# Seven-product blocks that add up in shared PSUM banks, in both column halves of three chunks out of eight

## The chip, the core and the metric

The kernel runs on one core of a Trainium2 chip, in one launch. The metric is device time in microseconds (us). Before the change three runs gave 2297.48, 2298.36 and 2298.86 us; the median is 2298.36 us.

Engine names are those of the profile: PE is TensorE (matrix products into PSUM), PEld its weight loads, DVE is VectorE, ACT is ScalarE, POOL is GpSimd, SP is the queue that starts the transfers from HBM. Nearly every instruction is recorded under one helper's line, L71, so the text goes by tile names.

## The reference, cut to what matters

A trunk of two layers on 256 tokens of width 2048: a mixer and a feed-forward block each, with residual sums. The change touches the two feed-forward blocks alone:

```
def squared_relu_mlp(h, w_up, w_down):
    u = jnp.einsum('bsd,df->bsf', h, w_up)
    return jnp.einsum('bsf,fd->bsd', jnp.square(jax.nn.relu(u)), w_down)
...
h = rms_norm(x, norm_ffn[layer])
x = x + squared_relu_mlp(h, w_up[layer], w_down[layer])
```

`w_up` is 2048 x 8192, `w_down` 8192 x 2048, all in float32.

## The kernel before

**Pieces.** All weights stream through the core once. The host-side list `plan` holds pieces of two row tiles (2 x 128 rows) by 512 columns, 512 KB each. SP loads a piece (`wraw`, four buffers, or `sraw`, from the shared pool of 29 slots). Float32 precision is made from three reduced products: ACT writes a rounded copy `whi` (`high`), DVE writes the rest `wlo` = raw - `whi` (`low`), and the PE adds up x_hi·w_hi, x_hi·w_lo and x_lo·w_hi. A plain piece is 12 matmuls of 512 columns (2 row tiles x 2 token halves x 3) into a pair of PSUM banks called `acc`.

**Order around a piece.** In step i of the loop in `run`, the queues get `low(i+2)` on DVE, the load of piece i+6 on SP, `high(i+3)` on ACT, `add(i+4)` on DVE (below), then what the piece before left behind (`pending`: an eviction), then side tasks that `tick` lets in, then the PE's piece i. There are four `wlo` buffers, so `low(j)` can't start until the PE is through with piece j-4: DVE is never more than some three pieces ahead. Engines take their queues in order.

**Feed-forward.** `up(i)` makes block i of 512 hidden columns (8 pieces; 16 blocks). `squared(i)` applies relu on ACT, turns the block with 8 PE transposes (`uT`) and squares it into `uf`. `operands(c)` splits blocks 2c and 2c+1 into `uh`/`ul` and makes two combinations of them, `s1` and `s2`, split into `sh`/`sl`. Chunk c (c = 0..7) multiplies the two blocks by 1024 rows of `w_down`. Column tiles 2 and 3 are plain: `down(c, 2)`, `down(c, 3)`, four pieces each, evicted by `add_stripe` into `res`.

**Seven products.** Column tiles 0 and 1 of chunks 0 to 6 go by a seven-product scheme (Winograd's form of Strassen's): the 2 x 2 blocks of token halves, hidden blocks and column tiles need seven products in place of eight. `Seven` gives 14 pieces, P1, P2, Q3, Q5, Q7, Q6, Q4 in two halves each, of 6 matmuls a piece into one bank, `sp`. Four of the seven weights are sums of raw blocks, made in place on DVE (`sraw<-sraw`, `add`). Each product is taken out of PSUM by one DVE addition (or, in chunk 0, an ACT copy), partly into the keeps `pq` and `q6`; after chunk 6 `together` combines these into `res` on DVE, and the first two column tiles of chunk 7 wait for that (`pre`). Chunk 7 is plain in all four column tiles.

**Plan.** Chunk c's stretch mixes its 14 seven-pieces into `up(2c+2)`, `down(c,2)`, `down(c,3)`, `up(2c+3)`, from the fifth of these pieces on. `operands(c)` waits for chunk c-1 to be through (`("seven", ...)`, `("rest", ...)`). So blocks 14 and 15 get their `uh`/`ul` only after the last piece of chunk 6, and `down(7, 0)` follows directly.

Of the kernel before, what the change touches and what calls it, by code (L numbers as in the profile page):

```python
# [7 lines left out]
F32 = mybir.dt.float32  # L8
# [3 lines left out]
OP = mybir.AluOpType  # L12
# [8 lines left out]
W = 512  # L21
# [19 lines left out]
def trunk(ctx: ExitStack, tc: tile.TileContext, x, norm_mix, norm_ffn, w_up, w_down, ab_w_in, ab_q_norm,  # L41
# [41 lines left out]
    def aux(name):  # L83
        return auxs.tile([128, W], F32, name=name, tag="aux")
# [150 lines left out]
    def unit(*a, **k):  # L235
# [1 line left out]

    SEVEN = (("P1", "11", None), ("P2", "21", None), ("Q3", "22", None), ("Q5", "11", "12"), ("Q7", "12", "22"),  # L240
             ("Q6", "11", "22"), ("Q4", "11", "21"))

    class Seven:


        def __init__(self, w, rows, c0, kts, operands, evict, needs, mark):
            self.w, self.rows, self.c0, self.operands, self.evict, self.needs, self.mark = \
                w, rows, c0, operands, evict, needs, mark
            self.halves = kts // KC
            self.raw = {}  # L250
            self.pieces = [(self, (p, h)) for p in range(7) for h in range(self.halves)]

        def fetch(self, p, h):
            _, block, other = SEVEN[p]
            b = block if other is None else "12" if p == 3 else None
            if b is not None:
                r, c = self.rows[int(b[0]) - 1] + h * KC, self.c0 + (int(b[1]) - 1) * W
                self.raw[b, h] = t = work.tile([128, KC, W], F32, name="sraw", tag="w4")
                nc.sync.dma_start(t, self.w[r * 128:(r + KC) * 128, c:c + W].rearrange("(k p) c -> p k c", p=128))

        def add(self, p, h):
            _, block, other = SEVEN[p]
            if other is not None:
                t = self.raw[block, h]
                V.tensor_tensor(t, t, self.raw[other, h], op=OP.add)

        def source(self, p, h):
            return self.raw[SEVEN[p][1], h]

    def run():  # L270
        todo = plan
# [50 lines left out]
        high(AHEAD)  # L322
        nc.sync.dma_start(cst[:, C_TRI:], shapes[:, C_TRI:])
        pending = []
        before = ps = sp = None
        kept, held = [], []
        for i, (u, c) in enumerate(todo):
            if i:
# [7 lines left out]
            hi, lo = parts.pop(i)  # L336
            if isinstance(u, Seven):
                p, h = c
                name = SEVEN[p][0]
                if p in u.needs and h == 0:  # L340
                    need(u.needs[p])
                if h == 0:
                    sp = aux("sp")
                xh, xl, t0 = u.operands(name)
                tick(True)
                for k in range(KC):
                    q = h * KC + k
                    wh, wl = xh[:, q, t0:t0 + 128], xl[:, q, t0:t0 + 128]
                    PE.matmul(sp, wh, hi[:, k], start=q == 0, stop=False)
                    PE.matmul(sp, wh, lo[:, k], start=False, stop=False)  # L350
                    PE.matmul(sp, wl, hi[:, k], start=False, stop=q == u.halves * KC - 1)
                if h == u.halves - 1:
                    pending.append(lambda u=u, name=name, sp=sp: u.evict(name, sp))
                    if p == 6:
                        done.add(u.mark)
                continue
# [238 lines left out]
                last(t, j)  # L595
        free(ps)

    def residual_unit(w, ktiles, j, needs={}, nm=None, last=None, pre=None, mark=None):
        def after(ps):
            if pre is not None:  # L600
                need(pre)
# [323 lines left out]
    def mlp(layer, nm, nxt, last=None):  # L925
# [21 lines left out]

        def operands(c):

            if c:  # L950
                yield from until(("seven", layer, c - 1))
                yield from until(("rest", layer, c - 1))
            for i in (2 * c, 2 * c + 1):
                yield from until(("uf", layer, i))
                u[i] = slot("uh"), slot("ul")
                split(u[i][0], u[i][1], uf[i])
                done.add(("u", layer, i))
                yield 2
# [20 lines left out]
        def up(i):  # L979
            return Unit([(wu, i * W, W)], nm.ktiles(), lambda ps: after_up(i, ps),  # L980
                        needs=nm.needs() if i == 0 else {}).pieces

        def down(c, j):
            kts = [(4 * (2 * c + b) + k, (lambda b=b, k=k: u[2 * c + b] + (k,))) for b in range(2) for k in range(4)]
            end = c == NC - 1
            return residual_unit(wd, kts, j, {4 * b: ("u", layer, 2 * c + b) for b in range(2)},
                                 nxt if end else None, last if end else None,
                                 ("seven's sums", layer) if end and j < 2 else None,
                                 ("rest", layer, c) if j == NS - 1 else None).pieces


        keep = {}
        R = [[res[:, t, j * W:(j + 1) * W] for j in range(2)] for t in range(2)]

        def evict(c, name, ps):
            if c == 0 and name == "P1":
                keep["pq"], keep["q6"] = w4([128, 2, W], "pq"), w4([128, W], "q6")
                keep["P1"], keep["Q5"], keep["Q6"] = keep["pq"][:, 0], keep["pq"][:, 1], keep["q6"]
                V.tensor_tensor(R[1][0], R[1][0], R[1][1], op=OP.add)
            if name in keep and c == 0:  # L1000
                S.activation(keep[name], ps, AF.Copy)
            else:
                r = {"P2": R[0][0], "Q3": R[0][1], "Q4": R[1][0], "Q7": R[1][1]}.get(name)
                r = keep[name] if r is None else r
                V.tensor_tensor(r, ps, r, op=OP.add)
            if c == NC - 2 and name == "Q4":
                side(together(), ("seven's sums", layer))

        def together():
            P1, Q5, Q6 = keep["P1"], keep["Q5"], keep["Q6"]  # L1010
            V.tensor_tensor(R[0][0], P1, R[0][0], op=OP.add)
            V.tensor_tensor(P1, Q6, P1, op=OP.subtract)
            V.tensor_tensor(R[1][1], P1, R[1][1], op=OP.add)
            V.tensor_tensor(R[1][0], R[1][0], R[1][1], op=OP.subtract)
            yield 2
            V.tensor_tensor(P1, P1, Q5, op=OP.add)
            V.tensor_tensor(R[0][1], P1, R[0][1], op=OP.add)
            V.tensor_tensor(R[1][1], Q5, R[1][1], op=OP.add)
            yield 1

        def seven(c):
# [20 lines left out]

# [113 lines left out]
```

## Time and profile before

| what | us |
|---|---|
| median of three runs | 2298.36 |
| the profiled execution's own time | 2297.73 |
| its span, first to last instruction | 2295.9 |
| PE busy | 2277.0 |
| DVE busy | 1692.5 |
| ACT busy | 1239.9 |

The page gives busy times and shares; the granted PE clock was 0.998 of full speed on average. The feed-forward blocks begin at 510.54 us and 1615.88 us (the first matmul of `up(0)`); the first one's last piece begins at 1186.68 us. A chunk takes 86.2 us. In the timelines a row's first number is a start, the second a length; rows of PE overlap (a matmul lasts 0.39 us, the next starts 0.23 us after it), so for PE the differences of starts count, and for DVE too, where an instruction of 1.22 us is followed 1.14 us after its start.

### The profile page before, as it was taken

The numbers are of one execution on the slowest core, as the hardware profiler recorded it, in microseconds if no ns is written. First come the engines' busy times: TensorE is split into PE (matmuls) and PEld (weight loads), VectorE is DVE, ScalarE is ACT, GpSimd is POOL, SyncE is SP. The second block draws the span as 40 slices with busy tenths as digits, with TensorE's granted clock in tenths as the row PEclk, the third lists the DMA queues.
The fourth block names the chain that finished last, engine by engine and source line by source line (L and its number), as shares of the span: only waits on it lengthen the run. The fifth ranks groups of instructions, "written<-read, shape, count | busy, mean of one in ns | idle before, by whom it ended". The sixth has DMA issues, their size and how long they took to land.

```text
span 2295.9 us, 29951 instructions
## 1 busy us (share of the span) xinstructions
PE 2277.0 (99%) x11149; PEld 1898.3 (83%) x11149; DVE 1692.5 (74%) x2418; ACT 1239.9 (54%) x1561; POOL 8.4 (0%) x20
## 2 busy tenths in 40 slices
PE   8999999999999999999999999999999999999998
PEld 7998988888888888888788778778888888888887
DVE  6779976556787787787866766665577787787785
ACT  5565554445556556556454555555555555555553
POOL 1000000000000000000000000000000000000000
PEclk9999999999999999999999999999999999999999
DMA  7546565566556656656456455545756656656654
GB/s 232 166 139 193 174 186 173 191 186 222 187 176 223 187 177 222 188 177 222 145 177 190 148 162 160 173 156 178 221 163 217 206 164 217 205 164 218 204 165 145
DMA packets 229202, 424.73 MB, mean 185 GB/s; under 512 B 15620, under 2 KB 26160, under 8 KB 229056
## 3 DMA queue, kind: packets, MB, share of 16 engines
q1 hardware_dynamic: 218976, 416.34, 58.1%
q10 hardware_dynamic: 9568, 6.34, 0.9%
q8 instruction: 87, 1.43, 0.2%
q14 instruction: 59, 0.48, 0.1%
q0 software_dynamic: 512, 0.15, 0.0%
HBM read 420.64 MB, written 2.13 MB: 184 GB/s over the span
## 4 chain that ended last, share of the span: by engine, by line
PE 98%; DVE 1%; DMA 0%; ACT 0%; issue 0%; SPq 0%; ACTq 0%
PE acc L71 81%; PE sp L71 12%; PE uT L71 1%; PE sc L71 1%; PE o L71 1%; PE pT L71 1%; PE yp L71 1%; PE xT L71 1%; DMA wraw<-in_ab_w_in_dram 0%; DVE res L71 0%; PE qp L71 0%; DVE wlo L71 0%; PE yo L71 0%; PE kp L71 0%; PE yT L71 0%; PE xtok L71 0%
## 5 line engine op out<-in xcount | busy, mean ns | idle before, releaser
L71 ACT ACTIVATE whi<-wraw 128x1024 fp32r<-128x1024 f32 (+1 forms) x680 | 717.4, 1056 | 641.4 <-PE acc L71 518.1
L71 DVE TENSOR_TENSOR wlo<-wraw,whi 128x1024 fp32r<-128x1024 f32 (+1 forms) x680 | 823.4, 1216 | 314.7 <-PE acc L71 227.5
L71 PE MATMUL acc<-whi,hThi 128*128 128x512 f32 (+1 forms) x1632 | 645.5, 396 | 2.6 <-ACT hThi L71 2.6
L71 PE MATMUL acc<-whi,hTlo 128*128 128x512 f32 (+1 forms) x1632 | 634.7, 389 | 0.3 <-DVE hTlo L71 0.3
L71 PE MATMUL acc<-wlo,hThi 128*128 128x512 f32 (+1 forms) x1632 | 633.9, 388 | 0.0
L71 PEld LDWEIGHTS acc<-whi,hThi 128*128 128x128 f32 x1632 | 307.6, 189 | 68.1 <-issue 5.9
L71 PEld LDWEIGHTS acc<-whi,hTlo 128*128 128x128 f32 x1632 | 307.3, 188 | 64.7 <-DVE hTlo L71 0.9
L71 PEld LDWEIGHTS acc<-wlo,hThi 128*128 128x128 f32 x1632 | 307.8, 189 | 60.4 <-issue 1.0
L71 ACT ACTIVATE whi<-sraw 128x1024 fp32r<-128x1024 f32 x196 | 207.7, 1060 | 178.4 <-DVE sraw L71 151.1
L71 DVE TENSOR_TENSOR wlo<-sraw,whi 128x1024 fp32r<-128x1024 f32 x196 | 239.7, 1223 | 59.4 <-PE acc L71 30.4
L71 PE MATMUL acc<-whi,uh 128*128 128x512 f32 x576 | 228.7, 397 | 3.4 <-ACT uh L71 3.4
L71 PE MATMUL acc<-whi,ul 128*128 128x512 f32 x576 | 226.0, 392 | 1.7 <-DVE ul L71 1.7
L71 PE MATMUL acc<-wlo,uh 128*128 128x512 f32 x576 | 225.5, 391 | 0.0
L71 DVE TENSOR_TENSOR sraw<-sraw 128x1024 f32<-128x1024 f32 x112 | 136.6, 1220 | 0.0
L71 PEld LDWEIGHTS acc<-whi,ul 128*128 128x128 f32 x576 | 108.9, 189 | 25.7 <-DVE ul L71 2.6
L71 PEld LDWEIGHTS acc<-whi,uh 128*128 128x128 f32 x576 | 108.9, 189 | 25.4 <-ACT uh L71 3.8
L71 PEld LDWEIGHTS acc<-wlo,uh 128*128 128x128 f32 x576 | 109.0, 189 | 21.7
L71 PE MATMUL acc<-hThi,whi 128*128 128x256 f32 x384 | 112.3, 293 | 0.0
L71 PE MATMUL acc<-hThi,wlo 128*128 128x256 f32 x384 | 108.5, 283 | 0.0
L71 PE MATMUL acc<-hTlo,whi 128*128 128x256 f32 x384 | 108.5, 283 | 0.0
L71 PE MATMUL sp<-whi,sh 128*128 128x512 f32 x224 | 87.1, 389 | 0.0
L71 PE MATMUL sp<-wlo,sh 128*128 128x512 f32 x224 | 87.1, 389 | 0.0
(228 smaller groups left out, 2535.9 us busy)
## 6 DMA issues: line engine op xcount, KB each, us to landing
wraw<-in_w_up_dram SPq DMA_DIRECT2D x256, 512.0 KB, 3.7
wraw<-in_w_down_dram SPq DMA_DIRECT2D x144, 512.0 KB, 4.3
sraw<-in_w_down_dram SPq DMA_DIRECT2D x112, 512.0 KB, 5.9
wraw<-in_ab_w_in_dram SPq DMA_DIRECT2D x96, 512.0 KB, 3.7
wraw<-in_c_w_qkv_dram SPq DMA_DIRECT2D x96, 512.0 KB, 4.0
wraw<-in_ab_w_out_dram SPq DMA_DIRECT2D x48, 512.0 KB, 3.7
wraw<-in_c_w_o_dram SPq DMA_DIRECT2D x32, 512.0 KB, 3.7
wt<-cumd ACTq DMA_DIRECT2D x8, 512.0 KB, 6.5
```

The costliest lines, as they stand in the source:

```text
L71: return f(out, *a, **k)
```

## The change

**Signs and banks.** `s1` and `s2` are made with their signs turned, and the order of the products is P1, P2, Q6, Q7, Q5, Q4, Q3. P1, Q6, Q5 and Q3 add up in one PSUM bank ("a"), Q7 and Q4 in another ("c"); P2 has one of its own. After each product DVE adds the bank as it stands to a block of `res`, or subtracts it. The keeps, `together` and the wait `pre` are gone, and so are ACT's copies in chunk 0.

**Weight sums.** P2 brings three raw blocks in one go (SP), and its own step makes the sum 11+12; Q6 needs 11+12+22 in a new tile `t2`, Q7 12+22, Q4 21-sum. As before, a seven has eight sums (four, in two halves each); P1, Q5 and Q3 have none.

**Both halves.** In chunks 0, 2 and 4 a second seven takes column tiles 2 and 3, so these chunks have no plain `down`. To have enough other pieces, they get three `up` blocks, and chunks 1, 3 and 5 get one.

**Order.** In chunk 6's stretch both `up` blocks come ahead of the plain `down` pieces, and `operands(7)` waits only for its own last block. The new `mixed` spreads the seven-pieces evenly.

```diff
-    SEVEN = (("P1", "11", None), ("P2", "21", None), ("Q3", "22", None), ("Q5", "11", "12"), ("Q7", "12", "22"),
-             ("Q6", "11", "22"), ("Q4", "11", "21"))
+    SEVEN = (("P1", "a", "11"), ("P2", "b", "21"), ("Q6", "a", "t2"), ("Q7", "c", "12"), ("Q5", "a", "11"),
+             ("Q4", "c", "21"), ("Q3", "a", "22"))
+    LOADS = {"P1": ("11",), "P2": ("21", "12", "22")}
+    SUMS = {"P2": ("11", "11", "12"), "Q6": ("t2", "11", "22"), "Q7": ("12", "12", "22"), "Q4": ("21", "21", "t2")}
...
+        def fetch(self, p, h):
...
+            for b in LOADS.get(SEVEN[p][0], ()):
...
+        def add(self, p, h):
...
+            if SEVEN[p][0] in SUMS:
+                o, x, y = SUMS[SEVEN[p][0]]
+                x, y = self.raw[x, h], self.raw[y, h]
+                V.tensor_tensor(self.raw[o, h] if o != "t2" else self.tile(o, h), x, y, op=OP.add)
...
+        def evict(self, p):
+
+            name, b, _ = SEVEN[p]
+            t, j, op = {"P1": (0, 0, OP.add), "P2": (0, 0, OP.add), "Q6": (1, 0, OP.add), "Q7": (1, 1, OP.subtract),
+                        "Q5": (1, 1, OP.subtract), "Q4": (1, 0, OP.add), "Q3": (0, 1, OP.subtract)}[name]
+            r = self.to[t][j]
+            V.tensor_tensor(r, r, self.bank[b], op=op)
...
-                if h == 0:
-                    sp = aux("sp")
+                new = b not in u.bank
+                if new:
+                    u.bank[b] = aux("sp")
+                sp = u.bank[b]
...
-                    PE.matmul(sp, wh, hi[:, k], start=q == 0, stop=False)
+                    PE.matmul(sp, wh, hi[:, k], start=new and k == 0, stop=False, skip_group_check=True)
...
-            if c:
-                yield from until(("seven", layer, c - 1))
-                yield from until(("rest", layer, c - 1))
+            if 0 < c < NC - 1:
+                for k in marks[c - 1]:
+                    yield from until(k)
+            if c == NC - 1:
+                yield from until(("uf", layer, 2 * c + 1))
...
-            V.tensor_tensor(s1[:, :, n], a1[:, :, o], s1[:, :, o], op=OP.subtract)
+            V.scalar_tensor_tensor(s1[:, :, n], a1[:, :, o], -1.0, s1[:, :, o], op0=OP.mult, op1=OP.subtract)
...
+        def mixed(rest, s, start):
+
+            n, k = len(s), 0
+            for i, x in enumerate(rest):
+                while k < n and i >= start + (len(rest) - start) / n * k:
+                    plan.append(s[k])
+                    k += 1
+                plan.append(x)
+            plan.extend(s[k:])
...
         plan.extend(up(0) + up(1))
-        for c in range(NC - 1):
-            rest = up(2 * c + 2) + down(c, 2) + down(c, 3) + up(2 * c + 3)
-            s = seven(c)
-            for k, x in enumerate(rest):
-                while s and k >= 4.5 + (len(rest) - 4.5) / 14 * (14 - len(s)):
-                    plan.append(s.pop(0))
-                plan.append(x)
-            plan.extend(s)
+        for c, (ups, both) in enumerate((((2, 3, 4), 1), ((5,), 0), ((6, 7, 8), 1), ((9,), 0), ((10, 11, 12), 1),
+                                         ((13,), 0), ((14, 15), 0))):
+            p = [up(i) for i in ups]
+            d = [] if both else [down(c, 2), down(c, 3)]
+            order = p[:1] + d + p[1:] if c < NC - 2 else p + d
+            mixed(sum(order, []), seven(c, 0) + (seven(c, 2) if both else []), 4.5)
```

How the instructions of the built programs stand, at two places.

DVE in chunk 0 of layer 0, from the splits of the two combinations on. Before, 12 rows from there:

```order
L71 TENSOR_TENSOR sl<-s_5336,sh 128x1024
L71 TENSOR_TENSOR sl<-s_5337,sh 128x1024
L71 TENSOR_TENSOR wlo<-wraw,whi 128x1024
L71 TENSOR_TENSOR wlo<-sraw,whi 128x1024
L71 TENSOR_TENSOR res<-res 128x512
L71 TENSOR_TENSOR wlo<-wraw,whi 128x1024
L71 TENSOR_TENSOR wlo<-sraw,whi 128x1024
L71 TENSOR_TENSOR wlo<-wraw,whi 128x1024 x2
L71 TENSOR_TENSOR wlo<-sraw,whi 128x1024
L71 TENSOR_TENSOR res<-sp,res 128x512
L71 TENSOR_TENSOR wlo<-wraw,whi 128x1024
L71 TENSOR_TENSOR wlo<-sraw,whi 128x1024
```

and in the changed kernel, from the row that stands just ahead of the same splits:

```order
L71 TENSOR_TENSOR sraw<-sraw 128x1024
L71 TENSOR_TENSOR sl<-s_5345,sh 128x1024
L71 TENSOR_TENSOR sl<-s_5346,sh 128x1024
L71 TENSOR_TENSOR wlo<-wraw,whi 128x1024
L71 TENSOR_TENSOR wlo<-sraw,whi 128x1024
L71 TENSOR_TENSOR sraw<-sraw 128x1024
L71 TENSOR_TENSOR res<-res,sp 128x512
L71 TENSOR_TENSOR wlo<-wraw,whi 128x1024
L71 TENSOR_TENSOR sraw<-sraw 128x1024
L71 TENSOR_TENSOR wlo<-sraw,whi 128x1024 x2
L71 TENSOR_TENSOR sraw<-sraw 128x1024
L71 TENSOR_TENSOR res<-res,sp 128x512
```

Four sums `sraw<-sraw` now stand around the splits and the first evictions of the seven, where the kernel before has none in its twelve rows.

DVE at the end of chunk 6 of layer 0. Before, from the last seven-product on:

```order
L71 TENSOR_TENSOR res<-sp,res 128x512
L71 TENSOR_TENSOR res<-pq,res 128x512
L71 TENSOR_TENSOR pq<-q_5412,pq 128x512
L71 TENSOR_TENSOR res<-pq,res 128x512
L71 TENSOR_TENSOR res<-res 128x512
L71 TENSOR_TENSOR wlo<-wraw,whi 128x1024
L71 TENSOR_TENSOR pq<-pq 128x512
L71 TENSOR_TENSOR res<-pq,res 128x512 x2
L71 TENSOR_TENSOR ul<-uf,uh 128x1024 x2
L71 TENSOR_TENSOR wlo<-wraw,whi 128x1024 x4
```

and in the changed kernel, from the eviction ahead of the first `ul` of block 14 on:

```order
L71 TENSOR_TENSOR res<-res,sp 128x512
L71 TENSOR_TENSOR wlo<-sraw,whi 128x1024
L71 TENSOR_TENSOR wlo<-wraw,whi 128x1024
L71 TENSOR_TENSOR ul<-uf,uh 128x1024
L71 TENSOR_TENSOR wlo<-wraw,whi 128x1024
L71 TENSOR_TENSOR res<-acc,res 128x512 x2
L71 TENSOR_TENSOR wlo<-sraw,whi 128x1024
L71 TENSOR_TENSOR res<-res,sp 128x512
L71 TENSOR_TENSOR ul<-uf,uh 128x1024
L71 TENSOR_TENSOR wlo<-wraw,whi 128x1024
L71 TENSOR_TENSOR wlo<-sraw,whi 128x1024
L71 TENSOR_TENSOR wlo<-wraw,whi 128x1024 x3
```

The two `ul`, which stood last, behind all of `together`, now stand between pieces of chunk 6, and the seven instructions of `together` are gone.

PE at the same place, before:

```order
L71 MATMUL acc<-wlo,hThi 128x512
L71 MATMUL acc<-whi,hTlo 128x512
L71 MATMUL uT<-cst,relu 128x128 x8
L71 MATMUL acc<-whi,uh 128x512
L71 MATMUL acc<-wlo,uh 128x512
```

and in the changed kernel, around the second set of block 15's transposes:

```order
L71 MATMUL sp<-wlo,sh 128x512
L71 MATMUL sp<-whi,sl 128x512
L71 MATMUL uT<-cst,relu 128x128 x4
L71 MATMUL acc<-whi,uh 128x512
L71 MATMUL acc<-wlo,uh 128x512
```

The transposes of the last block stood right ahead of the first product that needs them; now they stand between pieces of chunk 6, whose plain products use blocks 12 and 13.

## Rows read from the trace of the kernel before

**Rows 1.** The profile page: its first line, and the line of part 1 with busy time, share of the span and instructions of each engine.

```profile
span 2295.9 us, 29951 instructions
...
PE 2277.0 (99%) x11149; PEld 1898.3 (83%) x11149; DVE 1692.5 (74%) x2418; ACT 1239.9 (54%) x1561; POOL 8.4 (0%) x20
```

**Rows 2.** The waits of PE over the whole span, longest in total first: us in total, times, longest.

```profile
PE acc L71 <- ACT uh L71: 3.4, 2, 1.7
...
PE acc L71 <- ACT hThi L71: 2.6, 2, 2.3
PE acc L71 <- DVE ul L71: 1.7, 2, 0.9
```

**Rows 3.** Timeline of PE in chunk 6 of layer 0: the first matmul of a plain piece, of the seven-piece two plain pieces later, and of the next plain piece.

```profile
1108.19 0.39 PE L71 MATMUL acc<-whi,hThi 128*128 128x512 f32 x1
...
1113.63 0.39 PE L71 MATMUL sp<-whi,sh 128*128 128x512 f32 x1
...
1114.99 0.39 PE L71 MATMUL acc<-whi,hThi 128*128 128x512 f32 x1
```

**Rows 4.** Timeline of PE at the end of chunk 6, layer 0 (the last matmul of the last `up` piece, the transposes, the first products of chunk 7) and, after the dots, of layer 1 (the last matmul of the last `up` piece and, later, the twelfth product of chunk 7).

```profile
1136.52 0.39 PE L71 MATMUL acc<-whi,hTlo 128*128 128x512 f32 x1
...
1137.69 0.98 PE L71 MATMUL uT<-cst,relu 128*128 128x128 f32 x7 [0.35 <-ACT relu L71]
1140.36 0.50 PE L71 MATMUL acc<-whi,uh 128*128 128x512 f32 x1 [1.68 <-ACT uh L71]
...
1141.95 0.80 PE L71 MATMUL acc<-whi,ul 128*128 128x512 f32 x1 [0.86 <-DVE ul L71]
...
1145.09 0.39 PE L71 MATMUL acc<-whi,uh 128*128 128x512 f32 x1
...
2241.86 0.39 PE L71 MATMUL acc<-whi,hTlo 128*128 128x512 f32 x1
...
2251.04 0.39 PE L71 MATMUL acc<-whi,ul 128*128 128x512 f32 x1
```

**Rows 5.** Windows at the end of chunk 6, layer 0: length, busy us (and count) of PE, PEld, DVE, ACT, POOL, granted PE clock, DMA share, GB/s.

```profile
1136.70:1141.70 5.00, 2.25 (x11) 1.18 (x10) 4.93 (x7) 4.36 (x7) 0.00 (x0) 0.99 0.38 129
1141.70:1145.10 3.40, 3.15 (x8) 2.49 (x9) 2.47 (x3) 0.49 (x1) 0.00 (x0) 0.51 0.08 27
```

**Rows 6.** The same columns for chunks 1 and 2 of layer 0 together.

```profile
623.00:795.70 172.70, 172.70 (x779) 143.04 (x778) 136.27 (x131) 96.63 (x101) 0.00 (x0) 1.00 0.62 196
```

**Rows 7.** Timeline of DVE in the sums' stretch of chunk 1, layer 0.

```profile
663.88 0.68 DVE L71 TENSOR_TENSOR res<-sp,res 128x512 f32<-128x512 f32 x1
664.48 1.22 DVE L71 TENSOR_TENSOR wlo<-wraw,whi 128x1024 fp32r<-128x1024 f32 x1
665.61 1.22 DVE L71 TENSOR_TENSOR wlo<-sraw,whi 128x1024 fp32r<-128x1024 f32 x1
666.75 1.22 DVE L71 TENSOR_TENSOR sraw<-sraw 128x1024 f32<-128x1024 f32 x1
667.88 1.22 DVE L71 TENSOR_TENSOR wlo<-wraw,whi 128x1024 fp32r<-128x1024 f32 x1
669.17 1.22 DVE L71 TENSOR_TENSOR wlo<-sraw,whi 128x1024 fp32r<-128x1024 f32 x1
```

**Rows 8.** Timeline of DVE at the start of chunk 0, layer 0 (543 to 565 us).

```profile
543.47 1.22 DVE L71 TENSOR_TENSOR wlo<-wraw,whi 128x1024 fp32r<-128x1024 f32 x1
544.61 0.69 DVE L71 TENSOR_TENSOR s<-uf 128x512 f32<-128x512 f32 x1
...
547.14 1.22 DVE L71 TENSOR_TENSOR wlo<-sraw,whi 128x1024 fp32r<-128x1024 f32 x1
548.28 1.22 DVE L71 TENSOR_TENSOR wlo<-wraw,whi 128x1024 fp32r<-128x1024 f32 x1
550.04 2.36 DVE L71 TENSOR_TENSOR sl<-s,sh 128x1024 fp32r<-128x1024 f32 x2 [0.55 <-ACT sh L71]
552.32 1.22 DVE L71 TENSOR_TENSOR wlo<-wraw,whi 128x1024 fp32r<-128x1024 f32 x1
...
558.71 2.58 DVE L71 TENSOR_TENSOR wlo<-wraw,whi 128x1024 fp32r<-128x1024 f32 x2 [1.16 <-issue]
...
564.32 0.69 DVE L71 TENSOR_TENSOR res<-sp,res 128x512 f32<-128x512 f32 x1 [0.31 <-PE sp L71]
```

**Rows 9.** Timeline of PE in the same chunk: first matmuls of pieces (the first is the seven-piece P1, second half).

```profile
551.88 0.39 PE L71 MATMUL sp<-whi,uh 128*128 128x512 f32 x1
...
553.24 0.39 PE L71 MATMUL acc<-whi,hThi 128*128 128x512 f32 x1
...
562.76 0.39 PE L71 MATMUL sp<-whi,uh 128*128 128x512 f32 x1
...
564.48 0.48 PE L71 MATMUL acc<-whi,uh 128*128 128x512 f32 x1
...
567.67 0.48 PE L71 MATMUL acc<-whi,uh 128*128 128x512 f32 x1
...
570.51 0.39 PE L71 MATMUL sp<-whi,sh 128*128 128x512 f32 x1
```

**Rows 10.** The page's list of DMA issues, the seven's raw blocks: count, KB each, median us from issue to landing.

```profile
sraw<-in_w_down_dram SPq DMA_DIRECT2D x112, 512.0 KB, 5.9
```

**Rows 11.** A window of 4 us in chunk 1, layer 0, in which seven-pieces and plain pieces load side by side; columns as in Rows 5.

```profile
644.00:648.00 4.00, 4.00 (x19) 3.34 (x18) 2.45 (x2) 2.86 (x4) 0.00 (x0) 1.00 0.93 314
```

More of the change, by code (lines that the diff above doesn't have):

```diff
@@ L243, in trunk, with __init__ @@
     class Seven:
-        def __init__(self, w, rows, c0, kts, operands, evict, needs, mark):
-            self.w, self.rows, self.c0, self.operands, self.evict, self.needs, self.mark = \
-                w, rows, c0, operands, evict, needs, mark
+        def __init__(self, w, rows, c0, kts, operands, to, needs, mark):
+            self.w, self.rows, self.c0, self.operands, self.to, self.needs, self.mark = \
+                w, rows, c0, operands, to, needs, mark
             self.halves = kts // KC
-            self.raw = {}
+            self.raw, self.bank = {}, {}
@@ L251, in __init__, with tile @@
             self.pieces = [(self, (p, h)) for p in range(7) for h in range(self.halves)]
+        def tile(self, b, h):
+            self.raw[b, h] = t = work.tile([128, KC, W], F32, name="sraw", tag="w4")
+            return t
         def fetch(self, p, h):
-            _, block, other = SEVEN[p]
-            b = block if other is None else "12" if p == 3 else None
-            if b is not None:
+            for b in LOADS.get(SEVEN[p][0], ()):
                 r, c = self.rows[int(b[0]) - 1] + h * KC, self.c0 + (int(b[1]) - 1) * W
-                self.raw[b, h] = t = work.tile([128, KC, W], F32, name="sraw", tag="w4")
-                nc.sync.dma_start(t, self.w[r * 128:(r + KC) * 128, c:c + W].rearrange("(k p) c -> p k c", p=128))
+                nc.sync.dma_start(self.tile(b, h),
+                                  self.w[r * 128:(r + KC) * 128, c:c + W].rearrange("(k p) c -> p k c", p=128))
@@ L324, in run @@
         pending = []
-        before = ps = sp = None
+        before = ps = None
         kept, held = [], []
@@ L596, in add_stripe, with residual_unit @@
         free(ps)
-    def residual_unit(w, ktiles, j, needs={}, nm=None, last=None, pre=None, mark=None):
+    def residual_unit(w, ktiles, j, needs={}, nm=None, last=None, mark=None):
         def after(ps):
-            if pre is not None:
-                need(pre)
             add_stripe(ps, j, last)
@@ L981, in up @@
                         needs=nm.needs() if i == 0 else {}).pieces
+        marks = {c: [] for c in range(NC)}
         def down(c, j):
@@ L985, in down, with seven @@
             end = c == NC - 1
+            marks[c].append(("down", layer, c, j))
             return residual_unit(wd, kts, j, {4 * b: ("u", layer, 2 * c + b) for b in range(2)},
[L987 to L1021, printed above, removed]
+                                 nxt if end else None, last if end else None, marks[c][-1]).pieces
+        def seven(c, j):
             def parts(name):
@@ L1025, in parts @@
                 return (sums[c][k] if i else u[2 * c + k]) + (t,)
-            return Seven(wd, (8 * c, 8 * c + 4), 0, 4, parts, lambda name, ps: evict(c, name, ps),
+            marks[c].append(("down", layer, c, j))
+            return Seven(wd, (8 * c, 8 * c + 4), j * W, 4, parts,
+                         [[res[:, t, (j + i) * W:(j + i + 1) * W] for i in range(2)] for t in range(2)],
                          {0: ("u", layer, 2 * c), 1: ("u", layer, 2 * c + 1), 2: ("sums", layer, c)},
-                         ("seven", layer, c)).pieces
-        plan.extend(up(0) + up(1))
-        for c in range(NC - 1):
-            rest = up(2 * c + 2) + down(c, 2) + down(c, 3) + up(2 * c + 3)
-            s = seven(c)
-            for k, x in enumerate(rest):
-                while s and k >= 4.5 + (len(rest) - 4.5) / 14 * (14 - len(s)):
-                    plan.append(s.pop(0))
-                plan.append(x)
-            plan.extend(s)
+                         marks[c][-1]).pieces
+        def mixed(rest, s, start):
[6 more added lines that the diff above has]
+            plan.extend(s[k:])
+        plan.extend(up(0) + up(1))
+        for c, (ups, both) in enumerate((((2, 3, 4), 1), ((5,), 0), ((6, 7, 8), 1), ((9,), 0), ((10, 11, 12), 1),
[4 more added lines that the diff above has]
+            mixed(sum(order, []), seven(c, 0) + (seven(c, 2) if both else []), 4.5)
         for j in range(NS):
```

20 lines of the change are left out of this document (8 added, 12 removed).

## Prediction

> **What bounds the kernel now.** First the page's busy times: the PE is busy for 2277.0 of 2295.9 us, DVE for 74%, ACT for 54% [rows 1]. Matmuls overlap in the record, so next its waits and its pace. Waits in the feed-forward blocks are few: 3.4 us on ACT's `uh` and 1.7 us on DVE's `ul`, twice each [rows 2]. The pace is even: two plain pieces, 24 matmuls, take 1113.63 - 1108.19 = 5.44 us, or 0.2267 us a matmul; a seven-piece of 6 takes 1.36 us [rows 3]. So wherever DVE, ACT and the loads keep ahead, the count of matmuls sets the time. DVE has 136.3 us of work in two chunks of 172.7 us [rows 6]: room, but not much.
>
> **The change part by part.** The sums go against the profiled execution (2297.73 us, 1.8 us around its span); the median of the runs is 0.6 us above it, and the forecast is given against the median, 2298.36 us.
>
> *Six more sevens.* In chunks 0, 2 and 4 of both layers, `down(c,2)` and `down(c,3)` (8 pieces x 12 = 96 matmuls) become 14 pieces x 6 = 84. That is 12 fewer six times, 72 x 0.2267 = 16.3 us, all on the PE, which is the path. Transposes, loaded bytes and `up` pieces stay as many.
>
> *The end of each block.* Before, blocks 14 and 15 get their operands after the last piece of chunk 6. The PE makes the 8 transposes, stops 1.68 us for `uh` and 0.86 us for `ul`, and its next matmuls run at half speed: the granted clock is 0.51, the lower of its two levels (1.2 of 2.4 GHz), from 1141.7 to 1145.1 us, after the engine had been busy for 2.25 of the 5.0 us ahead [rows 4, 5]. From the last `hTlo` matmul (1136.52) to the tenth product (1145.09) are 8.57 us. At full pace this is 10 x 0.2267 = 2.27 us, plus 8 transposes. Those cost 0.95 us where they stand among pieces: three pieces around them take 1.72, 3.19 and 2.84 us in place of 1.36, 2.72 and 2.72 [rows 9]. So 8.57 - 3.22 = 5.35 us are lost. In layer 1, 2241.86 to 2251.04 are 9.18 us for 12 x 0.2267 + 0.95 = 3.67: 5.51 us lost [rows 4]. In the changed order both `ul` stand among pieces of chunk 6, the second one eight pieces ahead of the first product that reads it, and `together` is gone. What hides them is chunk 6's plain pieces, 2.72 us of PE each. So 10.9 us go. If only the stops went and the PE had to wait for the loads there, the half-speed stretches would remain, 2 x 1.7; I see nothing that would make it wait, since chunk 6's stretch has a single seven.
>
> *DVE's bill.* An instruction on 1024 columns takes 1.14 us from start to start, one on 512 columns 0.60 us [rows 7]. A double and a single chunk get, against two chunks before: 6 more `low`, 8 more sums, 3 more evictions, 14 x 1.14 + 3 x 0.60 = 17.8 us. With the 136.3 us of before, that is 154.1 us in 172.7 - 2.7 = 170.0 us, or 91%. On average it fits. The scaled second forms of `s1` and `s2` have as many elements, so I take them at nothing. ACT gets 30 conversions more in all, under 40 us of its idle 1056 us: hidden.
>
> *Where it doesn't fit.* At a chunk's start DVE has to make `ul`, `s1`, `s2` and `sl`, and now the sums of P2 and Q6 follow at once, in place of P1, P2 and Q3 without any. Chunk 0 in its own times [rows 8, 9]: DVE is free for the first extra sum at 544.61. Sum to 545.75, the four `s` (2.53) to 548.28, two `low` to 550.56, sum to 551.70 (this covers the 0.55 us wait for `sh`), two `sl` (2.28) to 553.98, `low` to 555.12. The piece that wants it starts 1.36 us after 553.24, because a seven-piece has taken a plain one's place, and its second matmul reads it at 554.83: the PE stops for 0.3 us. Then come `low`, sum, eviction, `low`, sum, two `low`, sum, eviction, `low`: 8 x 1.14 + 2 x 0.60 = 10.3 us, 10.5 with 0.15 us extra for a `low` behind its own sum [rows 7], against two plain and three seven-pieces on the PE, 9.5 us: 1.0 us more. That makes about 1.35 us, twice in the kernel: +2.7 us. In chunks 1 to 5 the order puts the two `ul` ahead of the `low` of the fourth and the fifth piece (before: the fourth and the seventh), and `sl` ahead of the seventh (before: the tenth); ACT has the first `uh` ahead of the relu. So the bill comes some three pieces earlier. The same account keeps DVE ahead by 2.0 us at the least in chunks 1, 3 and 5 and by 1.2 us in 2 and 4: no stop. The extra may be off by 1 us a chunk: 0 to +8 us.
>
> *Loads.* P2 brings six blocks within a few pieces. At the 314 GB/s that a busy stretch moves [rows 11], 512 KB take 1.7 us and six 10 us; the row for one is 5.9 us to landing [rows 10]. DVE's sum for the second half needs the fifth, 8.4 us after the first starts. The order issues them behind the `low` four or five pieces ahead of their sum, with plain pieces and the operand work between, some 12 us. Price 0; if late, about 2 us a seven, within the bound above.
>
> *Shared banks.* A bank is read by DVE and then written on. The eviction starts 0.31 us after the product and takes 0.69 us [rows 8]; the bank's next product is at least four pieces later, 6.8 us or more. Price 0.
> The Trainium skill ("Perfetto Trace Analysis", section "Matmuls") speaks against this: independent groups should rotate through different PSUM banks, so that the evacuation of one overlaps the next group's matmuls. By that rule each reuse would stop the PE; it is the last rival below.
>
> **Sum.** -16.3 - 10.9 + 2.7 = -24.5 us: 2298.4 - 24.5 = 2273.9, say 2274 us. With no stops at all it is 2271.2 us.
>
> **The rivals.**
> *Stops that pull the clock down.* The short stops of chunk 0 come in all six double chunks, and each brings a stretch at half speed like that in [rows 5], 3.4 us that lose 1.7 us. 6 x (1.35 + 1.7) = 18.3 us in place of 2.7: 2289.5 us. For it: DVE is at 91%. Against it: the fall came after 2.75 idle us of 5.0, not after one.
> The Trainium skill ("TensorE: Matmul & The Clock Gate", section "A second HAM failure mode: psum-queue depth-cycling") tells of a kernel that cycles through banks, whose small stops between groups made the clock go up and down; by that rule this rival would be likelier than I put it.
>
> *Operands come late everywhere (slower).* What happens at chunk 7 before (products at the PE before `uh` and `ul` are there) happens at the start of all 14 mixed chunks, since chunk c still waits for all of chunk c-1 and an `up` may end its stretch. The price is [rows 4]'s 5.4 us: 14 x 5.4 = 75.6, 2298.4 - 27.2 + 75.6 = 2347 us. It is slower by more than 0.2% from (27.2 + 4.6) / 5.4, six such stops, on. Against it: P1 stands at the sixth place of the stretch, and the order has both `ul` ahead of the fifth piece's `low`.
>
> *DVE becomes the bound.* If waits between ACT and DVE cost 13% on its 154.1 us, a pair of chunks lasts 174 us, six pairs give back 6 x 4 = 24 us, and the kernel stays within 0.2%, near 2296 us. For it: DVE waits on `sh` [rows 8]. Against it: away from the sums, two `low` (2.28 us) stand against 4.08 us of PE for a plain and a seven-piece.
>
> *A bank can't be written while it is read.* Twenty sevens reuse a bank four times each; if nothing lay between, 80 x (0.31 + 0.69) = 80 us: 2351 us. It decides only where less than 1.0 us lies between, and the order shows no such place.
>
> **How the numbers follow.** Forecast case (2270 to 2279 us) 0.64; clock rival and what lies between (2279 to 2293) 0.23; DVE as the bound 0.05; late operands 0.04; banks 0.02; below 2270 us 0.02. About 0.2% (4.6 us) is what a measurement of this kernel can tell from no change. Faster: 0.64 + 0.23 + 0.02 = 0.89; within 0.2%: 0.05; slower: 0.06. The range reaches from 2270 (no stops, 2271.2, less a us of scatter) to 2289 (most of the clock rival), and leaves out under 0.2.
>
> **What would show it.** 11,077 PE records in place of 11,149; PE's waits on `uh` and `ul` gone and no 0.5 in the clock near the end of either block; DVE near 90% in the double chunks; small waits of `sp` or `acc` on `wlo` at the start of chunk 0, and none longer than 1.5 us. Wrong would be: waits on `wlo` in every double chunk, half-speed stretches inside the blocks, `sp` waiting on `res`, or DVE waiting on `sraw` loads.

## The result and the profile after

Four runs of the changed kernel gave 2273.37 to 2274.24 us, median 2273.84, beside 2298.09 us (four runs of before): a ratio of 0.9894, 95% interval 0.9877 to 0.9911. The forecast was 2274 us.

The page of the changed kernel: span and busy times [rows 1], then the groups of the weight sums and of the evictions of sevens, then the loads of the seven's raw blocks [rows 10].

```profile
span 2271.6 us, 29997 instructions
...
PE 2257.2 (99%) x11077; PEld 1881.9 (83%) x11077; DVE 1784.1 (79%) x2510; ACT 1268.0 (56%) x1591; POOL 8.4 (0%) x20
...
L71 DVE TENSOR_TENSOR sraw<-sraw 128x1024 f32<-128x1024 f32 x160 | 194.8, 1217 | 1.5 <-DMA sraw<-in_w_down_dram 1.5
...
L71 DVE TENSOR_TENSOR res<-res,sp 128x512 f32<-128x512 f32 x140 | 95.3, 681 | 9.2 <-PE sp L71 9.2
...
sraw<-in_w_down_dram SPq DMA_DIRECT2D x160, 512.0 KB, 8.3
```

72 PE records are gone and DVE has 91.6 us more. A raw block takes 8.3 us to landing in place of 5.9, and still DVE waited for one only once, 1.5 us.

PE's waits, in the layout of [rows 2], and under them the line on `relu` of the kernel before:

```profile
PE acc L71 <- DVE wlo L71: 1.7, 4, 0.6
...
PE uT L71 <- ACT relu L71: 0.5, 2, 0.2
```

```profile
PE uT L71 <- ACT relu L71: 0.7, 2, 0.4
```

The lines on `uh` and `ul` are gone, and the one on `wlo` is new. A wait of the transposes on `relu` was there before too, at the two ends [rows 4]; now it lies in chunk 0. The other waits in the view, but for 0.2 us on `pT`, lie in the first 30 us of the kernel.

Windows of the changed kernel, columns as in [rows 5]: chunks 2 and 3 of layer 0 together (a double and a single chunk, the counterpart of [rows 6]), then 40 us around the end of chunk 6.

```profile
704.76:874.46 169.70, 169.70 (x765) 140.57 (x764) 152.47 (x148) 101.73 (x107) 0.00 (x0) 1.00 0.61 199
```

```profile
1095.00:1135.00 40.00, 40.00 (x182) 33.15 (x181) 31.02 (x30) 22.93 (x24) 0.00 (x0) 1.00 0.48 151
```

The pair of chunks lasts 169.70 us (forecast 170.0), with 152.5 us of DVE (forecast 154.1). Before, a pair lasted 2 x 86.21 = 172.42 us, from the first seven-product of a chunk to that of the chunk after the next; the window of [rows 6] is 0.28 us longer than that, which makes up most of the forecast's 0.3 us too much. At the end of chunk 6 PE has no gap, and the clock stays at its upper level.

Chunk 0 is the only place where PE stops inside the blocks. Timeline of PE there: first matmul of a plain piece, its second, first of the next piece; the same once more; then the transposes.

```profile
553.42 0.39 PE L71 MATMUL acc<-whi,hThi 128*128 128x512 f32 x1
554.04 0.50 PE L71 MATMUL acc<-wlo,hThi 128*128 128x512 f32 x1 [0.23 <-DVE wlo L71]
...
556.67 0.39 PE L71 MATMUL sp<-whi,uh 128*128 128x512 f32 x1
...
563.49 0.39 PE L71 MATMUL acc<-whi,hThi 128*128 128x512 f32 x1
564.48 0.50 PE L71 MATMUL acc<-wlo,hThi 128*128 128x512 f32 x1 [0.60 <-DVE wlo L71]
...
567.11 0.39 PE L71 MATMUL sp<-whi,sh 128*128 128x512 f32 x1
...
568.50 0.33 PE L71 MATMUL uT<-cst,relu 128*128 128x128 f32 x1
569.08 0.55 PE L71 MATMUL uT<-cst,relu 128*128 128x128 f32 x3 [0.25 <-ACT relu L71]
569.38 0.48 PE L71 MATMUL acc<-whi,hThi 128*128 128x512 f32 x1
```

The two pieces last 3.25 and 3.62 us in place of 2.72: 0.53 and 0.90 us lost. The seven-piece with four transposes lasts 569.38 - 567.11 = 2.27 us, where 1.36 + 0.36 is what such a pair takes without a wait [rows 9]: 0.55 us lost. DVE in the same stretch, and ACT ahead of the transposes:

```profile
549.37 1.22 DVE L71 TENSOR_TENSOR sraw<-sraw 128x1024 f32<-128x1024 f32 x1
550.50 2.35 DVE L71 TENSOR_TENSOR sl<-s,sh 128x1024 fp32r<-128x1024 f32 x2
552.77 1.22 DVE L71 TENSOR_TENSOR wlo<-wraw,whi 128x1024 fp32r<-128x1024 f32 x1
...
563.21 1.22 DVE L71 TENSOR_TENSOR wlo<-wraw,whi 128x1024 fp32r<-128x1024 f32 x1
...
565.48 1.22 DVE L71 TENSOR_TENSOR sraw<-sraw 128x1024 f32<-128x1024 f32 x1
```

```profile
566.81 1.06 ACT L71 ACTIVATE whi<-sraw 128x1024 fp32r<-128x1024 f32 x1 [1.99 <-DVE sraw L71]
567.78 1.24 ACT L71 ACTIVATE relu<-acc,rs 128x512 f32<-128x512 f32 x2
```

DVE runs without a gap, and each late `wlo` ends just ahead of the matmul that waits (553.99 for 554.04). ACT's `whi` stands in its queue 1.99 us for DVE's sum, which ends at 566.70; the relu stands behind it, and the transposes wait for the relu. So late sums reach PE a second way, through ACT. Layer 1 reads alike (waits of 0.23, 0.60 and 0.25).

**Where the time went.** From the first matmul of chunk 0 to that of the next, 532.07 to 640.31 us, are 108.24 us; without loss it is 105.25 + 0.95 = 106.20 (three sets of transposes in place of two). So 2.0 us are lost in each layer. (Chunk 0 comes after `up(0)` and `up(1)`. In the kernel before, `up(0)` begins at 487.84 and 1593.19 us; the 510.54 and 1615.88 us given for it ahead of the prediction are the first matmuls of `up(1)`.) The sum by rows: -16.3 (matmuls), -5.4 and -5.5 (ends), +4.0 (chunk 0) = -23.2 of the span's -24.3. The other 1.1 to 1.2 us lie ahead of 52 us, which the change doesn't touch: the first transposes of block 0, with the same work ahead of them, begin 1.18 us earlier in the profiled run after (the first row is before). Then the window of 15 to 25 us, before, and the same window after:

```profile
513.26 0.60 PE L71 MATMUL uT<-cst,relu 128*128 128x128 f32 x4
```

```profile
512.08 0.60 PE L71 MATMUL uT<-cst,relu 128*128 128x128 f32 x4
```

```profile
15.00:25.00 10.00, 7.35 (x43) 7.07 (x43) 6.16 (x12) 8.08 (x21) 0.00 (x0) 0.83 0.93 308
```

```profile
15.00:25.00 10.00, 7.63 (x55) 6.99 (x54) 6.55 (x13) 8.60 (x21) 0.00 (x0) 1.00 0.93 309
```

The profiled run before had a stretch at the lower clock there, the one after had none. That isn't the whole of it: over the twelve profiled runs of this document the same transposes begin at 512.08 to 514.15 us, and in the run with one seven a chunk (experiment 3) at 513.59 us without such a stretch. So these 1.2 us are scatter of the start, and what makes it vary stays open.

### The profile page after: what moved, and what is told of

Same layout as the page of the kernel before. It is cut to its first block, busy times and chain, and to the rows that moved or that the text cites. A ratio compares the mean times of both kernels' runs of the same rounds, so it can differ in the third digit from the quotient of the medians.

```text
span 2271.6 us, 29997 instructions
## 1 busy us (share of the span) xinstructions
PE 2257.2 (99%) x11077; PEld 1881.9 (83%) x11077; DVE 1784.1 (79%) x2510; ACT 1268.0 (56%) x1591; POOL 8.4 (0%) x20
## 4 chain that ended last, share of the span: by engine, by line
PE 97%; DVE 1%; ACT 1%; DMA 0%; issue 0%; SPq 0%; DVEq 0%; ACTq 0%
PE acc L71 75%; PE sp L71 16%; PE uT L71 1%; PE sc L71 1%; PE o L71 1%; PE pT L71 1%; PE yp L71 1%; PE xT L71 1%; DVE wlo L71 0%; DVE sraw L71 0%; DMA wraw<-in_ab_w_in_dram 0%; PE qp L71 0%; DMA res<-in_x_dram 0%; ACT whi L71 0%; PE yo L71 0%
## 5 line engine op out<-in xcount | busy, mean ns | idle before, releaser
L71 DVE TENSOR_TENSOR wlo<-wraw,whi 128x1024 fp32r<-128x1024 f32 (+1 forms) x632 | 765.0, 1214 | 262.5 <-PE acc L71 188.1
L71 ACT ACTIVATE whi<-sraw 128x1024 fp32r<-128x1024 f32 x280 | 296.1, 1060 | 213.1 <-DVE sraw L71 136.3
L71 DVE TENSOR_TENSOR wlo<-sraw,whi 128x1024 fp32r<-128x1024 f32 x280 | 340.6, 1220 | 58.9 <-PE acc L71 44.1
L71 DVE TENSOR_TENSOR sraw<-sraw 128x1024 f32<-128x1024 f32 x160 | 194.8, 1217 | 1.5 <-DMA sraw<-in_w_down_dram 1.5
L71 PE MATMUL acc<-whi,uh 128*128 128x512 f32 x384 | 151.5, 394 | 0.0
L71 PE MATMUL acc<-whi,ul 128*128 128x512 f32 x384 | 149.7, 390 | 0.0
L71 PE MATMUL acc<-wlo,uh 128*128 128x512 f32 x384 | 149.6, 389 | 0.0
L71 PE MATMUL sp<-whi,sl 128*128 128x512 f32 x320 | 124.6, 389 | 0.0
L71 DVE TENSOR_TENSOR res<-res,sp 128x512 f32<-128x512 f32 x140 | 95.3, 681 | 9.2 <-PE sp L71 9.2
L71 PE MATMUL sp<-whi,ul 128*128 128x512 f32 x240 | 93.4, 389 | 0.0
```

What stands on the lines that cost most here:

```text
L71: return f(out, *a, **k)
```

## The experiments

Each was timed beside the kernel before (medians 2298.69 us for the first four, 2297.39 for the next four, 2297.87 for the last two). "As changed" is 2273.84 us.

**1. The ends alone**, in the kernel before:

```diff
-            if c:
+            if c == NC - 1:
+                yield from until(("uf", layer, 2 * c + 1))
+            elif c:
...
-            rest = up(2 * c + 2) + down(c, 2) + down(c, 3) + up(2 * c + 3)
+            d = down(c, 2) + down(c, 3)
+            rest = up(2 * c + 2) + d + up(2 * c + 3) if c < NC - 2 else up(2 * c + 2) + up(2 * c + 3) + d
```

> The kernel before, with one part of the change: in chunk 6 of both layers the two up blocks come ahead of the plain down pieces, and operands(7) waits only for the transposed block 15. Sevens, banks, keeps, together and its wait stay. Theory (the end term of the prediction, 5.35 + 5.51 us lost to the stops on uh and ul and to the half-speed stretch behind them, goes with the order alone): 2298.1 - 10.9 = 2287.2 us, no PE wait on uh or ul, no 0.5 in the clock near the ends. Rival (together, which still stands on DVE where chunk 7 begins, and the wait on it keep a stop there): about half of it, 2292 us or more. Rival (the loads are what is late there, so the half-speed stretch stays): 2298.1 - 10.9 + 3.4 = 2290.6 us.

Measured: 2286.76 us, ratio 0.9950 (0.9937 to 0.9964): -11.9 us. No wait on `uh` or `ul`, and no fall of the clock before the last us of the kernel, though `together` still stands where it did. The end term is there by order alone. In the profiled run the first transposes of block 0 begin 0.7 us earlier than before (512.54 us), and from there on it is shorter by 10.9 us, which is the term.

**2. All but the ends**, in the changed kernel:

```diff
-            if 0 < c < NC - 1:
+            if c:
...
-            if c == NC - 1:
-                yield from until(("uf", layer, 2 * c + 1))
...
-            order = p[:1] + d + p[1:] if c < NC - 2 else p + d
+            order = p[:1] + d + p[1:]
```

> The changed kernel with chunk 6's old order and operands(7) waiting for all of chunk 6; sevens, banks and the doubled chunks as changed. Theory (the ends are a term of their own): 2273.8 + 10.9 = 2284.7 us, with waits on uh and ul again. Rival (together's seven DVE instructions were a good part of that stop, and they are gone here): 2277 to 2281 us.

Measured: 2284.32 us, +10.5. PE's waits in this kernel:

```profile
PE acc L71 <- ACT uh L71: 3.4, 2, 1.7
...
PE acc L71 <- DVE ul L71: 0.5, 1, 0.5
```

The stop on `uh` is as long as it was [rows 2]; those on `ul`, 0.9 us twice before, are one of 0.5 us. The last `hTlo` matmul and the tenth product of chunk 7, in both layers:

```profile
1129.38 0.39 PE L71 MATMUL acc<-whi,hTlo 128*128 128x512 f32 x1
...
1137.19 0.39 PE L71 MATMUL acc<-whi,uh 128*128 128x512 f32 x1
...
2227.79 0.39 PE L71 MATMUL acc<-whi,hTlo 128*128 128x512 f32 x1
...
2235.91 0.39 PE L71 MATMUL acc<-whi,uh 128*128 128x512 f32 x1
```

These are 7.81 and 8.12 us where the prediction takes 3.22 without loss: 4.6 and 4.9 us lost in place of 5.4 and 5.5. So order is worth some 9.5 of the 10.9 us here, and 1.4 us go with something else that the change does. That `together` no longer stands on DVE there would fit; no run takes it out by itself. The rival, by which it was a good part of the stop, falls.

**3. One seven a chunk**, everything else as changed:

```diff
-        for c, (ups, both) in enumerate((((2, 3, 4), 1), ((5,), 0), ((6, 7, 8), 1), ((9,), 0), ((10, 11, 12), 1),
-                                         ((13,), 0), ((14, 15), 0))):
+        for c, (ups, both) in enumerate([((2 * c + 2, 2 * c + 3), 0) for c in range(NC - 1)]):
```

> The changed kernel with one seven in each of chunks 0 to 6, two up blocks and both plain down tiles in each: signs, shared banks, order of products and chunk 6's order as changed. Theory (72 matmuls come back, 16.3 us; the stops at the start of chunk 0 need the dense seven-pieces of a double chunk and go, 4.0 us): 2273.8 + 16.3 - 4.0 = 2286.1 us. Rival (the sums at chunk 0's start stop the PE with one seven too): 2290.1 us. Rival (the shared banks cost something that the double chunks' gain hides, 0.3 us at each of 28 reuses or more): under 2286 + (-8), that is 2278 us, cannot be; above 2291 us would speak for it.

Measured: 2286.61 us, +12.8 (forecast +12.3), with no wait on `wlo` or `relu`. The kernel with the ends alone (2286.76) has separate banks, keeps and `together`; this one has none of them and takes the same time. So the shared banks and the turned signs cost nothing here and gain nothing by themselves. What they are made for, by the code, is that a second seven needs no keeps; no run has a second seven with keeps of its own. (A seven reuses a bank four times, so this kernel has 56 reuses and not the 28 of the last rival.)

**4. Chunk 0 without its sums:**

```diff
-            if SEVEN[p][0] in SUMS:
+            if SEVEN[p][0] in SUMS and self.mark[2:] != (0, 0):
...
-            return self.raw[SEVEN[p][2], h]
+            b = SEVEN[p][2]
+            return self.raw["22" if b == "t2" and self.mark[2:] == (0, 0) else b, h]
```

> The changed kernel without the eight weight sums of chunk 0's first seven in both layers (it takes raw blocks in their place, so that seven computes something else; every product, load and eviction is there). Theory (the sums among chunk 0's operand work make DVE late, and that makes all three stops, 0.53, 0.90 and 0.57 us in each layer): 2273.8 - 4.0 = 2269.8 us, no PE wait on wlo or relu there. Rival (the stop at the transposes is ACT's own, not DVE's): 2273.8 - 2.9 = 2271.0 us with the wait on relu still there. Rival (the operand splits ul, s and sl alone make DVE late): 2273.8 us.

Measured: 2270.01 us, -3.8. All three stops are gone, the one on `relu` too: the rival by which that stop is ACT's own falls.

**5. A later start in chunk 0:**

```diff
-            mixed(sum(order, []), seven(c, 0) + (seven(c, 2) if both else []), 4.5)
+            mixed(sum(order, []), seven(c, 0) + (seven(c, 2) if both else []), 4.5 if c else 8)
```

> The changed kernel, whose chunk 0 (both layers) begins to mix in its seven-pieces at the eighth place of the stretch in place of 4.5: P1 and the sums of P2 and Q6 come some four plain pieces later, 2.72 us of PE each against 1.14 us of DVE. Theory (DVE is late only because the sums meet the operand work of the chunk's start): the stops go, 2273.8 - 4.0 = 2269.8 us. Rival (the seven-pieces get denser, 1.75 on each plain piece in place of 1.44, which is 94% of DVE by 1.14 and 0.60 us an instruction, and DVE is late further on): 2272 to 2276 us with waits on wlo inside chunk 0.

Measured: 2270.45 us, -3.4, ratio to before 0.9883 (0.9869 to 0.9896). The window of its chunk 0:

```profile
533.75:639.95 106.20, 106.20 (x481) 87.96 (x480) 94.09 (x89) 64.43 (x69) 0.00 (x0) 1.00 0.59 193
```

This is the 106.20 us without loss, with the same DVE work (94.1 us) as in the changed kernel's 108.24 (94.2 us); the first seven-piece comes after eight plain pieces in place of five. The profiled run starts late (its first transposes are at 513.76 us, with a stretch at the lower clock at 19.7 us); from there on it is 4.1 us shorter than as changed, which is the theory's 4.0. DVE was late for where its work stood, not for how much there was.

**6. Two sevens in every chunk:**

```diff
-        for c, (ups, both) in enumerate((((2, 3, 4), 1), ((5,), 0), ((6, 7, 8), 1), ((9,), 0), ((10, 11, 12), 1),
-                                         ((13,), 0), ((14, 15), 0))):
+        for c, (ups, both) in enumerate([((2 * c + 2, 2 * c + 3), 1) for c in range(NC - 1)]):
```

> The changed kernel with two sevens and two up blocks in each of chunks 0 to 6 of both layers, no plain down before chunk 7: 96 matmuls fewer. If the count of matmuls went on setting the time: -21.8, that is 2252 us. Theory (DVE is the bound from here on): a pair of chunks had 136.3 us of DVE with two sevens and has 152.5 with three, so 168.7 with four, against 167.0 us of matmuls; with DVE busy all the time 7 x 84.35 us a layer, 2260 us at the best, and with DVE's waits on ACT (2 to 4% of it) 2280 to 2305 us. PE waits on wlo all over the chunks.

Measured: 2312.04 us, slower than before: ratio 1.0066 (1.0053 to 1.0079). Chunk 2 of layer 0, then PE's longest waits over the whole span, then DVE's longest in this chunk:

```profile
707.58:794.91 87.33, 84.73 (x377) 68.85 (x376) 84.09 (x83) 52.74 (x57) 0.00 (x0) 1.00 0.58 193
```

```profile
PE acc L71 <- DVE wlo L71: 33.0, 28, 1.7
```

```profile
DVE ul L71 <- ACT uh L71: 2.6, 2, 1.9
```

A chunk has 83.5 us of matmuls and transposes and lasts 87.3, and DVE is busy for 96% of it and waits for PE nowhere in it: DVE is the bound. Its own 84.1 us are only 0.6 us more than PE's; the other 3.2 us of the 3.8 are DVE standing idle, 2.6 us of them for ACT's `uh`. The expectation was some 7 us too low at its upper end. It took the ends as kept, but with no plain `down` in chunk 6 the stop on `uh` is back (twice 1.7 us), and chunks 6 and 7 are 7.4 us longer than as changed in each layer. Six chunks give 6 x 87.3 - 512.1 = 11.7 us, and 2 x (11.7 + 7.4) = 38.2 us, the whole difference.

**7 and 8. Seven-pieces in twos, and a bank taken up at once.** The control, and the kernel that adds the change of places:

```diff
                 while k < n and i >= start + (len(rest) - start) / n * k:
-                    plan.append(s[k])
-                    k += 1
+                    m = 1 if k % 14 == 0 else 2
+                    plan.extend(s[k:min(k + m, n)])
+                    k += m
```

```diff
-    SEVEN = (("P1", "a", "11"), ("P2", "b", "21"), ("Q6", "a", "t2"), ("Q7", "c", "12"), ("Q5", "a", "11"),
-             ("Q4", "c", "21"), ("Q3", "a", "22"))
+    SEVEN = (("P1", "a", "11"), ("P2", "b", "21"), ("Q6", "a", "t2"), ("Q5", "a", "11"), ("Q7", "c", "12"),
+             ("Q4", "c", "21"), ("Q3", "a", "22"))
```

> The changed kernel with the seven-pieces put into the plan two at a time (second half of one product, first half of the next, back to back); the order of the products and the banks as changed, so two neighbours never share a bank. It is the control for the next kernel. Expected by all theories: 2273.8 us, give or take 4 us for the coarser mixing.

> The kernel with pairs, and Q5 and Q7 change places, so that Q6 and Q5 (bank a) and Q7 and Q4 (bank c) stand back to back: 2 of the reuses of each of the 20 sevens have nothing between them, 40 in all. Theory (a bank can't be written on before DVE has taken it out, which takes 0.31 + 0.69 us from the product's end, and up to 0.6 more where a sum stands ahead): 40 x 1.0 to 1.6, 2314 to 2338 us, with waits of sp on DVE's res. Rival (the PE goes on writing beside the read): 2273.8 us, no such waits. Rival (these stops also pull the clock down, 1.7 us each time): 40 x 2.7 and more, 2380 us.

Measured: 2277.22 us for the control (+3.4, of which 0.75 us in chunk 0 and 0.4 us in chunks 2 and 4 of each layer) and 2347.50 us with the reuse at once: 70.3 us for 40 reuses, 1.76 us each, against an expected 1.0 to 1.6. PE's waits of the latter, then PE and DVE at a short one:

```profile
PE sp L71 <- DVE res L71: 57.4, 40, 3.0
```

```profile
634.61 0.39 PE L71 MATMUL sp<-whi,sl 128*128 128x512 f32 x1
635.87 0.47 PE L71 MATMUL sp<-whi,uh 128*128 128x512 f32 x1 [0.87 <-DVE res L71]
```

```profile
635.03 0.69 DVE L71 TENSOR_TENSOR res<-res,sp 128x512 f32<-128x512 f32 x1
```

The product ends at 635.00, the eviction runs from 635.03 to 635.72, and the next matmul starts at 635.87, 1.03 us later than its pitch. Read like this, the 40 stops lose 0.94 to 3.14 us each and 63.8 us together, 1.6 us on average, which is the upper end of what was expected; the rest of the 1.76 us is the clock, below. Sixteen waits are under 0.9 us, with the eviction at the head of DVE's queue; the longer ones (1.6 to 1.9 us, two of 3.0) come where a sum, a `wlo` or both stand ahead of it. The profile infers the releaser from a semaphore, so this is a wait built into the program; what PE would do without it, no run shows. In the changed kernel no wait of `sp` on `res` is listed; the least that lies between two uses of a bank there is four pieces (36 matmuls, 8.0 us). In the kernels of experiments 5, 7, 9 and 10 it is three pieces (24 matmuls, 5.3 us), and no such wait is listed there either. The Trainium skill ("Perfetto Trace Analysis", section "Matmuls") has it that independent matmul groups should rotate through different PSUM banks; this kernel agrees where nothing lies between two uses, and the others show that three or four pieces between them do as well.

Of these 40 stops, four were followed by a stretch at the lower clock: both of 3.0 us, and two of the four of 1.93 us. Four times 3.41 us at 0.50 lose at most 6.8 us, and 63.8 + 6.8 = 70.6 us is close to the measured 70.3. One of the two longest stops, then the stretch behind it:

```profile
566.00:569.60 3.60, 1.25 (x6) 1.06 (x7) 3.34 (x4) 1.88 (x3) 0.00 (x0) 1.00 0.88 269
569.63:573.04 3.41, 3.41 (x10) 2.63 (x9) 2.36 (x2) 1.36 (x2) 0.00 (x0) 0.50 0.51 174
```

So the rival that counted 1.7 us of clock for each small stop falls: 36 stops of 0.8 to 1.9 us passed without one. The Trainium skill ("TensorE: Matmul & The Clock Gate", section "A second HAM failure mode: psum-queue depth-cycling") tells of a kernel whose small stops between groups made the clock swing; here that holds for four stops in forty, and for none of the shorter ones in the changed kernel.

**9 and 10. A fourth double chunk**, as a version that could beat both:

```diff
-        for c, (ups, both) in enumerate((((2, 3, 4), 1), ((5,), 0), ((6, 7, 8), 1), ((9,), 0), ((10, 11, 12), 1),
-                                         ((13,), 0), ((14, 15), 0))):
-            p = [up(i) for i in ups]
-            d = [] if both else [down(c, 2), down(c, 3)]
-            order = p[:1] + d + p[1:] if c < NC - 2 else p + d
-            mixed(sum(order, []), seven(c, 0) + (seven(c, 2) if both else []), 4.5)
+        stream = sum([up(i) for i in range(2, 2 * NC)], [])
+        for c, (n, both) in enumerate(((22, 1), (22, 1), (8, 0), (22, 1), (8, 0), (22, 1), (8, 0))):
+            p, stream = stream[:n], stream[n:]
+            d = [] if both else down(c, 2) + down(c, 3)
+            k = min(n, (n + len(stream)) % 8 or 8) if d else 0
+            mixed(p[:k] + d + p[k:], seven(c, 0) + (seven(c, 2) if both else []), 4.5 if c else 6.5)
```

> The changed kernel with a fourth double chunk in each layer: chunks 0, 1, 3 and 5 get two sevens and 22 up pieces, chunks 2, 4 and 6 one seven, 8 up pieces and both plain down tiles; chunk 0 mixes its seven-pieces in from place 6.5. 24 matmuls fewer than changed. Theory (the count of matmuls sets the time as long as DVE fits; a double chunk with 24 plain pieces had 95.27 us of DVE in 105.25, with 22 it has about 92.8 in 99.8, 93%): the stops of chunk 0 go too, 2273.8 - 4.0 - 5.4 = 2264.4 us. Rival (at 93% the order can't keep DVE ahead everywhere, and PE waits on wlo in several double chunks): 2268 to 2276 us.

> The same with chunk 0's seven-pieces from the eighth place. They are denser then, 2 on each plain piece: 5.3 us of DVE by 1.14 and 0.60 us an instruction against 5.44 us of PE. Theory: the start of chunk 0 has no stop, but its later part has: 2264.4 + 1 to 3 us. Rival (97% still fits): 2264.4 us.

Measured: 2264.51 us (ratio to before 0.9854, 0.9836 to 0.9872) with the start at 6.5, and 2265.27 us at 8 (0.9858, 0.9842 to 0.9874). Between them lie 0.8 us, and neither has a wait on `wlo` or `relu`: at 97% by this count DVE still kept ahead, and the expected 1 to 3 us of loss did not come (the profiled run at 8 had a stretch at the lower clock at 19 us, as the kernel before; that at 6.5 had none). A double chunk (chunk 1) of the first:

```profile
633.61:734.37 100.76, 100.76 (x458) 83.48 (x456) 91.98 (x88) 62.19 (x67) 0.00 (x0) 1.00 0.61 198
```

DVE is at 91% and PE without a gap. This is the fastest of these kernels, 9.3 us under the changed one.

## Why the prediction was right

- **The count of matmuls (-16.3).** Right: the pairs of chunks take 169.70 us in place of 172.42, -2.72 each where PE doesn't stop, and one seven a chunk gives 12.8 us back once chunk 0's stops are off (16.3 - 4.0 = 12.3).
- **The ends (-10.9).** Right in cause and size: 5.4 and 5.5 us by the stages of the two traces, -11.9 us alone (10.9 behind the start of the profiled run) and +10.5 us taken out (9.5 by its rows).
- **DVE at the start of chunk 0 (+2.7).** Right in place and mechanism, too small: +4.0. The two stops on `wlo`, put at 0.3 and 1.0 us, were 0.53 and 0.90; their sum, 1.43, is near the 1.35. What the step left out is the third stop, 0.55 to 0.6 us a layer: the account followed DVE's queue to the matmuls, and not through ACT, whose `whi` waits in order for DVE's sum while the relu waits behind it.
- **No stop in the other double chunks (0).** Right: no wait of PE there. The kernel with two sevens everywhere shows how near the bound was: at 96% DVE sets the pace, at 90 to 91% it does not.
- **Loads (0) and shared banks (0).** Right: one wait of 1.5 us on DVE that reached no matmul, and no wait of `sp`. For banks the experiment bounds it: 0.9 us or more where nothing lies between, none with three pieces between. The step misread one row: the 0.31 us that it put between a product and its eviction is DVE's idle time ahead of the eviction [rows 8]. From the record's end of the product (562.76 + 5 x 0.2267 + 0.39 = 564.28, [rows 9]) to the eviction are 0.04 us. The price of 0 rests on the distance and doesn't change with it.
- **The rivals.** Stops that pull the clock down: no low clock in the blocks; forty larger stops gave four stretches. Operands late everywhere: not seen. DVE the bound: true with two sevens in every chunk, and there its waits for ACT are most of the loss. Banks: their price is real and their place is not in this order.
- The forecast met the median within 0.2 us in part by two errors of opposite sign: 1.3 us too little in chunk 0, and about 1.2 us by which the start of the kernel was shorter in the profiled run after, which was luck.

## What to carry over

Cost a moved chain of work on every in-order queue that carries it: late DVE sums stopped PE through `wlo`, and once more through an ACT conversion that held up a relu. A queue that is busy for 90% of a stretch can still be without price if its dense work is spread: the same DVE work cost 2.0 us in one order and nothing in another. An accumulation bank can be read and written on without a price if some other pieces stand between (three were enough here); back to back each reuse stopped PE for 0.9 us or more, 1.6 us on average.

## What was not expected of the hardware

The granted clock was more tolerant of short stops than the price of the first rival supposed: in the kernel with 40 stops of 0.8 to 3.0 us it fell four times, each time to 0.50 for 3.41 us. The median landing time of raw blocks rose from 5.9 to 8.3 us in the kernel that asks for three of them at once, and no matmul waited for it.
